# An RWKV-7 and S5 block on one core: the scan's chain as full 128x128 products, its outputs made four chunks at once

## The chip, the cores and the metric

The kernel runs on one NeuronCore of a Trainium2 chip. A NeuronCore has a matrix engine, TensorE (PE in the profile; PEld is its loading of weights), and four more: VectorE (DVE), ScalarE (ACT), GpSimd (POOL) and SyncE (SP). Each works through its own list of instructions in order, and semaphores make one wait for another. DMA queues move data between device memory (DRAM) and the on-chip memory SBUF; matrix products land in a second memory, PSUM, which has eight banks. Each is organised in 128 partitions. The metric is the device time of one execution in microseconds (us); lower is better.

## The reference, cut to what matters

The block normalises x (2048 frames of 1024 channels), projects it, and runs two branches, an RWKV-7 recurrence (16 heads of 64) and an S5 state-space scan (32 groups). Both are gated, projected back, merged, projected once more and added to x. The change touches the RWKV-7 recurrence alone:

```python
def frame_step(S, inp):
    r_t, w_t, k_t, v_t, a_t, b_t = inp
    sa = jnp.einsum('bhij,bhj->bhi', S, a_t)
    S = S * w_t[:, :, None, :] + sa[..., None] * b_t[:, :, None, :] + v_t[..., None] * k_t[:, :, None, :]
    return S, jnp.einsum('bhij,bhj->bhi', S, r_t)
...
_, y = lax.scan(chunk_step, S0, (to_chunks(r), to_chunks(w), to_chunks(k),
                                  to_chunks(v), to_chunks(a), to_chunks(b)))
```

Here w is the decay of each frame and channel, a is minus the normalised key and b is that key times a learned rate.

## The kernel before

**Tiles.** Frames are cut into four blocks of 512 (`tb`), heads into eight pairs (`p`). One *unit* is a pair in a block: channels of the two heads on the 128 partitions (first head on 0 to 63, second on 64 to 127, `HS`), 512 frames along the free axis. There are 32 units; two neighbouring ones are the same pair in two blocks that follow each other. A unit has eight chunks of 64 frames.

**The chunk form.** Within a chunk the recurrence becomes matrix products. `prep1` (L677) makes, per unit, the exponentials of the summed log decay `eg` and of its negative `en`, the columns `BK` (keys divided by the decay) and `AR` (a and r times the decay; r's part in columns C to 2C, L733, on POOL), and `dec`, the decay over the whole chunk. `prep2` (L811) multiplies BK and AR into the matrices A (L822), which ACT and DVE scale and mask into `AT` (L828 to L830). Part of A is a unit triangular matrix per head and chunk; its inverse is needed. The 32x32 diagonal blocks go through DRAM (`ld`, L835, then `IX`, L840, so that all blocks lie side by side on the partitions) and are solved by 62 dependent DVE steps (`solve`, L869 to L877, L872 and L876 in turn). The result goes through DRAM again (`rd`, `R64`, L889 to L894), and the off-diagonal block is put together with 32x32 products (`pz` L908, `pr` L919). `BT`, the transposed BK (L846 to L849), and `SU`, which holds the values v and later the state (L851 to L862), are made in between.

**The scan.** `scan` (L925) then walks through the eight chunks, three steps each:

1. `px` (L934): AT times the current column block `cur` of SU, one full 128x128 product; DVE copies it to `rh`; ACT makes `us`, the state times the chunk's decay (L939).
2. The first half of the output `po` (L943, the state times r), then `pu` (L946), R64 times rh. Both are done head by head as 64x64 products on a quarter of the array each. DVE scales pu for the first head and ACT for the second, back into cur (L947, L948).
3. `pn` (L952), BT times cur, per head a product of 128 rows and 64 columns; two DVE instructions add it to us and write the state into the next chunk's block of SU (L960). Then the second half of the output (L962), AT times cur, per head.

All these operands are float32, and the profile shows each such product as two passes (two weight loads and two matmuls). The unit's output po is one PSUM bank; ACT copies it to `y` (L743, `post1`) at the next unit's start.

**The order of work.** Every engine's list is written by hand through generators. The loop at L1523 takes the units in turn; unit n's scan, the prep2 of unit n + 1, the prep1 of unit n + 2 (from slot 13 on) and the normalisation of unit n - 1 run side by side in 24 *slots* (L1543). A slot emits, in this order, one step of the scan, one step of prep2 (from slot 1 on), DVE work that was put off, then `sums` and prep1, and at last a group of six GEMM matmuls of the big projections (`stream`; slots 1, 9, 15 and 21 take twelve). Before, prep2 puts the two halves of A in slots 1 and 2, IX's loads and the first half of BT in slot 3, the second half of BT in slot 4, SU in slot 5, the solve in slots 6 to 16, pz in slot 22 and pr in slot 23. The solve's steps are woven between the other DVE instructions: `dve` is a wrapper that emits one solve step after every other DVE instruction while some are due (six per slot), so the listing shows many DVE instructions under L75, the line of the wrapper. `sums` (L759) sends row sums through DRAM in slots 4 and 7: `sd` (L771, L774), `cmp` (L777), `rkb`, all issued on SP, as ld, IX, rd and R64 are. Weight loads and several stores are issued on POOL.

PSUM tiles tagged "m" share three banks in turn; A, the transposes of BK, sums, SU's product, pz and pr take them in the order in which they are emitted. `u1` tiles have one buffer each, `up` tiles two, AR three.

Of the kernel before, what the change touches and what calls it, by code (L numbers as in the profile page):

```python
# [81 lines left out]
def tile_rwkv7_s5_block(  # L82
# [181 lines left out]
    if True:  # L264
# [412 lines left out]
        def prep1(p, tb):  # L677
# [50 lines left out]
            dve.tensor_copy(dec, c3(eg)[:, :, C - 1:C])  # L728
            ar = up.tile([P, NC, 2 * C], F32, tag="AR", bufs=3, name="AR" + n)
# [4 lines left out]
            u.update(rk=kh, dec=dec, dd=dd, bk=bk, ar=ar)  # L734
# [76 lines left out]
        def prep2(p, tb):  # L811
# [4 lines left out]
            ld = drx.tile([2, 2, NC, 32, 32], F32, tag="ld", name="ld" + n)  # L816
            for c2 in range(NC // 4):
# [19 lines left out]
            ix = u1.tile([P, 32, 32], F32, tag="IX", name="IX" + n)  # L837
# [3 lines left out]
            bt = up.tile([P, NC, 2, C], F32, tag="BT", name="BT" + n)  # L841
            for c2 in range(NC // 4):
                pb = psm.tile([P, 4, P], F32, tag="m", name=f"pb{n}_{c2}")
                cs_ = slice(4 * c2, 4 * c2 + 4)
                for i in range(4):
                    pe.transpose(pb[:, i, :], bk[:, 4 * c2 + i, 0:2, :].rearrange("p a s -> p (a s)"), ident)  # L846
                act.copy(bt[:, cs_, 0, :], pb[:, :, 0:C])
# [68 lines left out]
            for c in range(NC):  # L916
                for h in range(2):
                    s0 = 64 * h
                    pe.matmul(pr[s0:s0 + 32, 32 * c:32 * c + 32], zt[s0 + 32:s0 + 64, c, :], r64[s0 + 32:s0 + 64, c, 32:64], start=True, stop=True)  # L919
            for h in range(2):  # L920
                s0 = 64 * h
                act.copy(r64[s0:s0 + 32, :, 32:64], pr[s0:s0 + 32, 0:256].rearrange("p (c t) -> p c t", t=32))
            yield

        def scan(p, tb):  # L925
# [4 lines left out]
            for c in range(NC):  # L930
# [6 lines left out]
                us = sm.tile([P, C], F32, tag="us", name=f"us{n}_{c}")  # L937
# [3 lines left out]
                oc = po[:, c * C:(c + 1) * C]  # L941
                for h in range(2):
                    pe.matmul(oc[HS[h]], cur[HS[h], HS[h]], ar[HS[h], c, C:2 * C], start=True, stop=False)  # L943
                pu = pst.tile([P, 512], F32, tag="st", name=f"pu{n}_{c}")
                for h in range(2):
                    pe.matmul(pu[HS[h], 0:C], r64[HS[h], c, :], rh[HS[h], HS[h]], start=True, stop=True)  # L946
                dve.tensor_scalar(out=cur[0:64, 0:64], in0=pu[0:64, 0:C], scalar1=dd[0:64, c:c + 1], scalar2=None, op0=ALU.mult)  # L947
                act.activation(out=cur[64:128, 64:128], in_=pu[64:128, 0:C], func=AF.Copy, scale=dd[64:128, c:c + 1])  # L948
                yield
                pn = pst.tile([P, 512], F32, tag="st", name=f"pn{n}_{c}")  # L950
                for h in range(2):
                    pe.matmul(pn[HS[h], 0:C], bt[:, c, h, :], cur[:, HS[h]], start=True, stop=True)  # L952
                for h in range(2):
                    if c + 1 < NC:
                        nxt = su[HS[h], c + 1, HS[h]]
                    elif tb % 2 == 0:
                        nxt = U[p, tb + 1]["su"][HS[h], 0, HS[h]]
                    else:
                        nxt = ust[HS[h], p, :]
                    (raw_dve if h == 0 else dve).scalar_tensor_tensor(out=nxt, in0=pn[HS[h], 0:C], scalar=dec[HS[h]], in1=us[HS[h]], op0=ALU.mult, op1=ALU.add)  # L960
# [548 lines left out]
        with tc.manual_schedule():  # L1509
# [13 lines left out]
            for n in range(-1, NU + 1):  # L1523
# [180 lines left out]
```

## Time and profile before

| what | us |
|---|---|
| median of 3 runs | 2703.61 |
| lowest and highest | 2698.28 and 2709.49 |
| profiled execution, its own time | 2703.94 |
| span of that execution on the core | 2702.2 |
| first and last px of the scan (L934) | 144.9 and 2085.8 |

The scan's units run from 144.9 to 2085.8 us of the span; before them lies the first normalisation, behind them the S5 branch and the output projections, which the change leaves as they are. A row of the profile names line, engine, operation, out<-in by the program's names and shapes; behind the bar of a group stand busy time in us, mean ns of one, and idle time of the engine just before it with what ended it. In rows by order of time the first two columns are start and duration in us; matmuls overlap, so what one costs is read from the starts, not from the durations. The granted clock of PE was 0.991 of full speed in this execution. The rows themselves stand with the prediction.

### The profile page before, as it was taken

What the parts mean: (1) busy time and instruction counts of PE and PEld (TensorE: products, weight loads), DVE (VectorE), ACT (ScalarE), POOL (GpSimd) and SP (SyncE); (2) the same over time, 40 slices, a digit from 0 to 9 for tenths busy, and PEclk for the clock granted to TensorE, in tenths of its full rate; (3) what the DMA queues carried; (4) which work ended last, traced back from release to release, by engine and by line L of the source; (5) the groups of instructions that cost most, each with busy time, mean ns of one, the idle gap of its engine ahead of it and who ended that gap; (6) DMA issues with size and microseconds to landing.
All of it is one profiled execution on the core that took longest, in us unless ns stands there. A gap on an engine that the chain in (4) does not pass through costs nothing. (4 is left out here: it accounts for less than half of the span.)

```text
span 2702.2 us, 49102 instructions
## 1 busy us (share of the span) xinstructions
PE 2593.4 (96%) x17164; PEld 1970.5 (73%) x17164; DVE 1906.8 (71%) x5620; ACT 1413.6 (52%) x3547; POOL 613.0 (23%) x987
## 2 busy tenths in 40 slices
PE   6999999999999989999999999999989899899998
PEld 5777777777777766777777777777757777677787
DVE  5666777777667777767777767777768789645644
ACT  6456555555556676555555555555644444423321
POOL 2222212122222333222212122221332200111110
PEclk9999999999999999999999999999999999999999
DMA  3232333232333543333323233232466756845533
GB/s 112 79 81 69 97 82 98 72 91 77 89 85 86 138 126 102 92 79 85 85 78 90 80 94 88 78 93 78 133 178 188 218 152 165 247 164 172 169 104 98
DMA packets 256350, 303.54 MB, mean 112 GB/s; under 512 B 159745, under 2 KB 172134, under 8 KB 255078
## 3 DMA queue, kind: packets, MB, share of 16 engines
q1 hardware_dynamic: 210502, 150.94, 20.8%
q0 software_dynamic: 45600, 149.46, 18.7%
q8 instruction: 135, 2.21, 0.3%
q14 instruction: 113, 0.93, 0.1%
HBM read 219.91 MB, written 71.70 MB: 108 GB/s over the span
## 5 line engine op out<-in xcount | busy, mean ns | idle before, releaser
L948 ACT ACTIVATE SU<-pu,dd 64x64 f32<-64x64 f32 x256 | 79.0, 309 | 352.4 <-DVE SU L75 289.4
L872 DVE TENSOR_TENSOR TM<-RF,IX 128x60 f32<-128x60 f32 (+24 forms) x992 | 230.2, 232 | 27.7 <-DMA IX<-ld 5.4
L876 DVE TENSOR_TENSOR RF<-RF,TM 128x60 f32<-128x60 f32 (+24 forms) x992 | 223.9, 226 | 28.3
L939 ACT ACTIVATE us<-SU,dec 64x64 f32<-64x64 f32 x512 | 176.1, 344 | 66.1 <-DVE SU L960 58.2
L75 DVE TENSOR_TENSOR AT<-A,amask 64x256 f32<-64x256 f32 (+1 forms) x256 | 102.3, 419 | 115.0 <-ACT AT L828 109.5
L75 DVE TENSOR_SCALAR SU<-pu,dd 64x64 f32<-64x64 f32 x256 | 69.9, 273 | 112.0 <-PE pu L946 110.2
L828 ACT ACTIVATE AT<-A,dd 64x64 f32<-64x64 f32 x512 | 116.5, 302 | 38.5 <-PE A L822 36.5
L952 PEld LDWEIGHTS pn<-SU,BT 128*64 128x64 f32 x1024 | 56.1, 134 | 104.7 <-issue 38.8
L934 PEld LDWEIGHTS px<-SU,AT 128*128 128x128 f32 x512 | 94.7, 189 | 41.9 <-DVE SU L75 22.0
L960 DVE SCALAR_TENSOR_TENSOR SU<-pn,dec,us 64x64 f32<-64x64 f32 x240 | 65.5, 273 | 79.6 <-PE pn L952 77.6
L943 PEld LDWEIGHTS po<-AR,SU 64*64 64x64 f32 x1024 | 49.8, 131 | 97.0 <-issue 82.5
L75 DVE COPY rh<-px 128x128 f32<-128x128 f32 x256 | 73.9, 289 | 63.9 <-PE px L934 59.7
L488 PE MATMUL ppa<-yhi,whi_pa 128*128 128x512 f32 x256 | 114.1, 446 | 2.2 <-DVE sg L75 1.2
L934 PE MATMUL px<-SU,AT 128*128 128x128 f32 x512 | 100.3, 278 | 14.4 <-DVE SU L75 14.3
L488 PE MATMUL pmb<-hhi,whi_mb 128*128 128x512 f32 x256 | 111.7, 436 | 0.0
L488 PE MATMUL pma<-hhi,whi_ma 128*128 128x512 f32 x256 | 111.1, 434 | 0.0
L488 PE MATMUL pga<-hhi,whi_ga 128*128 128x512 f32 x256 | 110.9, 433 | 0.0
L488 PE MATMUL pk<-hhi,whi_k 128*128 128x512 f32 x256 | 110.8, 433 | 0.0
L488 PE MATMUL pr<-hhi,whi_r 128*128 128x512 f32 x256 | 110.5, 432 | 0.0
L488 PE MATMUL pv<-hhi,whi_v 128*128 128x512 f32 x256 | 109.7, 429 | 0.6 <-ACT carry L441 0.6
L490 PE MATMUL ppa<-yhi,wlo_pa 128*128 128x512 f32 x256 | 102.9, 402 | 2.6 <-DVE wlo_pa L75 2.6
L1662 PE MATMUL pout<-wohi,mhi 128*128 128x512 f32 x256 | 101.1, 395 | 2.5 <-ACT mhi L255 2.4
(374 smaller groups left out, 7980.0 us busy)
## 6 DMA issues: line engine op xcount, KB each, us to landing
IX<-ld SPq DMA_DIRECT2D x128, 128.0 KB
raw_pa<-in_p_a_dram POOLq DMA_DIRECT2D x64, 256.0 KB, 4.5
raw_mb<-in_w_in_dram POOLq DMA_DIRECT2D x50, 256.0 KB, 3.6
raw_r<-in_w_in_dram POOLq DMA_DIRECT2D x36, 256.0 KB, 3.7
raw_k<-in_w_in_dram POOLq DMA_DIRECT2D x36, 256.0 KB, 3.8
raw_v<-in_w_in_dram POOLq DMA_DIRECT2D x36, 256.0 KB, 3.4
raw_ga<-in_w_in_dram POOLq DMA_DIRECT2D x34, 256.0 KB, 3.5
ce<-cw SPq DMA_DIRECT2D x16, 514.0 KB
```

Of the source, the lines that this page charges most:

```text
L75: r = f(*a, **kw)
L488: pe.matmul(ps, hi[:, k, :], xhi[:, kk_, :], start=(kk_ == 0), stop=False)
L490: pe.matmul(ps, lo[:, k, :], xhi[:, kk_, :], start=False, stop=(kk_ == 7))
L828: act.activation(out=at[HS[h], c, 0, h, :], in_=pas[h][HS[h], i, 0:C], func=AF.Copy, scale=dd[HS[h], c:c + 1])
L872: raw_dve.tensor_tensor(out=tm[:, 0:na, 0:nt], in0=rf[:, 0:na, s:s + 1].to_broadcast([P, na, nt]), in1=ix[:, s:s + 1, s + 1:32].to_broadca ...
L876: raw_dve.tensor_tensor(out=rf[:, 0:na, s + 1:32], in0=rf[:, 0:na, s + 1:32], in1=tm[:, 0:na, 0:nt], op=ALU.add)
L934: pe.matmul(px[:, 0:P], at[:, c, 0].rearrange("p h t -> p (h t)"), cur, start=True, stop=True)
L939: act.activation(out=us[HS[h]], in_=cur[HS[h], HS[h]], func=AF.Copy, scale=dec[HS[h]])
L948: act.activation(out=cur[64:128, 64:128], in_=pu[64:128, 0:C], func=AF.Copy, scale=dd[64:128, c:c + 1])
L952: pe.matmul(pn[HS[h], 0:C], bt[:, c, h, :], cur[:, HS[h]], start=True, stop=True)
L960: (raw_dve if h == 0 else dve).scalar_tensor_tensor(out=nxt, in0=pn[HS[h], 0:C], scalar=dec[HS[h]], in1=us[HS[h]], op0=ALU.mult, op1=ALU.add)
L1662: pe.matmul(ps, mhi[:, k, js], whi[:, k, qs], start=(k == 0), stop=False)
```

## The change

- **pu and pn** become one full 128x128 product each, for both heads. R64 gets a block per head, [128, 8, 2, 64], with zeros outside the blocks; two fixed tiles, zeroed once at the start, take the place of the two buffers and of two POOL memsets per unit. DVE and ACT read the diagonal blocks of pu and pn.
- **The outputs** leave the scan. A new function `outs` makes them for four chunks in slot 22 and for the other four in slot 23, after prep2's step: first eight 64x64 products (the state half), then eight of 128x64, each as two passes. For this the state of every chunk must be kept: us, the state times the chunk's decay, goes into the a part of AR instead of a tile of its own, and r's part of AR is divided by that decay. `rdec` (copied on POOL in prep1) is the reciprocal; one POOL product over 128x512 in prep2, in slot 4, applies it.
- **prep2's order**: both halves of BT come first, in slot 1; the two halves of A move to slots 2 and 3, with ld; IX's loads and the POOL product are in slot 4. IX now shares BK's buffer.

```diff
+        r64s = [up.tile([P, NC, 2, C], F32, tag=f"R64{i}", bufs=1, name=f"R64{i}") for i in range(2)]
+        for t_ in r64s:
+            pool.memset(t_, 0.0)
...
+            rdec = sm.tile([P, NC, 1], F32, tag="rdec", name="rdec" + n)
+            pool.tensor_copy(rdec, c3(en)[:, :, C - 1:C])
...
+            bt = up.tile([P, NC, 2, C], F32, tag="BT", name="BT" + n)
+            for c2 in range(NC // 4):
+                pb = psm.tile([P, 4, P], F32, tag="m", name=f"pb{n}_{c2}")
...
+            yield
             for c2 in range(NC // 4):
                 pas = [psm.tile([P, 4, 2 * C], F32, tag="m", name=f"A{n}_{c2}_{h}") for h in range(2)]
...
-            ix = u1.tile([P, 32, 32], F32, tag="IX", name="IX" + n)
+            ix = u1.tile([P, 32, 32], F32, tag="BK", name="IX" + n)
             ldf = ld.rearrange("h b c s t -> (h b c) s t")
             for q in range(4):
                 sp.dma_start(out=ix[32 * q:32 * q + 32], in_=ldf)
-            bt = up.tile([P, NC, 2, C], F32, tag="BT", name="BT" + n)
-            for c2 in range(NC // 4):
...
-                yield
+            pool.tensor_tensor(out=ar[:, :, C:2 * C], in0=ar[:, :, C:2 * C], in1=u["rdec"].to_broadcast([P, NC, C]), op=ALU.mult)
+            yield
...
-            r64 = up.tile([P, NC, C], F32, tag="R64", name="R64" + n)
+            r64 = r64s[units.index((p, tb)) % 2]
...
-                    sp.dma_start(out=r64[s0:s0 + 32, :, 32 * b:32 * b + 32], in_=rd[h, b].rearrange("c a q t -> (a q) c t"))
-                pool.memset(r64[64 * h + 32:64 * h + 64, :, 0:32], 0.0)
+                    sp.dma_start(out=r64[s0:s0 + 32, :, h, 32 * b:32 * b + 32], in_=rd[h, b].rearrange("c a q t -> (a q) c t"))
...
-                us = sm.tile([P, C], F32, tag="us", name=f"us{n}_{c}")
+                us = ar[:, c, 0:C]
...
-                oc = po[:, c * C:(c + 1) * C]
-                for h in range(2):
-                    pe.matmul(oc[HS[h]], cur[HS[h], HS[h]], ar[HS[h], c, C:2 * C], start=True, stop=False)
                 pu = pst.tile([P, 512], F32, tag="st", name=f"pu{n}_{c}")
-                for h in range(2):
-                    pe.matmul(pu[HS[h], 0:C], r64[HS[h], c, :], rh[HS[h], HS[h]], start=True, stop=True)
...
+                pe.matmul(pu[:, 0:P], r64[:, c].rearrange("p h t -> p (h t)"), rh, start=True, stop=True)
...
-                for h in range(2):
-                    pe.matmul(pn[HS[h], 0:C], bt[:, c, h, :], cur[:, HS[h]], start=True, stop=True)
+                pe.matmul(pn[:, 0:P], bt[:, c].rearrange("p h j -> p (h j)"), cur, start=True, stop=True)
...
-                for h in range(2):
-                    pe.matmul(oc[HS[h]], cur[:, HS[h]], at[:, c, 1, h, :], start=False, stop=True)
...
+        def outs(p, tb, cs):
+            u = U[p, tb]
+            ar, at, su, po = (u[k] for k in ("ar", "at", "su", "po"))
+            for c in cs:
+                for h in range(2):
+                    pe.matmul(po[HS[h], c * C:(c + 1) * C], ar[HS[h], c, 0:C], ar[HS[h], c, C:2 * C], start=c == cs[0], stop=False)
+            for c in cs:
+                for h in range(2):
+                    pe.matmul(po[HS[h], c * C:(c + 1) * C], su[:, c, HS[h]], at[:, c, 1, h, :], start=False, stop=c == cs[-1])
...
+                    if sc is not none and slot in (22, 23):
+                        outs(*units[n], range(4 * (slot - 22), 4 * (slot - 21)))
```

More of the change, by code (lines that the diff above doesn't have):

```diff
@@ L733, in prep1 @@
             pool.tensor_tensor(out=ar[:, :, C:2 * C], in0=c3(r), in1=c3(eg), op=ALU.mult)
-            u.update(rk=kh, dec=dec, dd=dd, bk=bk, ar=ar)
+            u.update(rk=kh, dec=dec, rdec=rdec, dd=dd, bk=bk, ar=ar)
             DONE["r"] += 1
@@ L816, in prep2 @@
             ld = drx.tile([2, 2, NC, 32, 32], F32, tag="ld", name="ld" + n)
+            bt = up.tile([P, NC, 2, C], F32, tag="BT", name="BT" + n)
+            for c2 in range(NC // 4):
+                pb = psm.tile([P, 4, P], F32, tag="m", name=f"pb{n}_{c2}")
+                cs_ = slice(4 * c2, 4 * c2 + 4)
+                for i in range(4):
+                    pe.transpose(pb[:, i, :], bk[:, 4 * c2 + i, 0:2, :].rearrange("p a s -> p (a s)"), ident)
+                act.copy(bt[:, cs_, 0, :], pb[:, :, 0:C])
+                for h in range(2):
+                    act.copy(bt[HS[1 - h], cs_, 1, :], pb[HS[h], :, C:2 * C])
+            yield
             for c2 in range(NC // 4):
@@ L840, in prep2 @@
                 sp.dma_start(out=ix[32 * q:32 * q + 32], in_=ldf)
-            bt = up.tile([P, NC, 2, C], F32, tag="BT", name="BT" + n)
-            for c2 in range(NC // 4):
[L843 to L847, printed above, removed]
-                for h in range(2):
-                    act.copy(bt[HS[1 - h], cs_, 1, :], pb[HS[h], :, C:2 * C])
-                yield
+            pool.tensor_tensor(out=ar[:, :, C:2 * C], in0=ar[:, :, C:2 * C], in1=u["rdec"].to_broadcast([P, NC, C]), op=ALU.mult)
+            yield
             su = up.tile([P, NC, P], F32, tag="SU", name="SU" + n)
@@ L901, in prep2 @@
             for h in range(2):
-                dve.transpose(t11[64 * h:64 * h + 32], r64[64 * h:64 * h + 32, :, 0:32])
+                dve.transpose(t11[64 * h:64 * h + 32], r64[64 * h:64 * h + 32, :, h, 0:32])
                 yield
@@ L918, in prep2 @@
                     s0 = 64 * h
-                    pe.matmul(pr[s0:s0 + 32, 32 * c:32 * c + 32], zt[s0 + 32:s0 + 64, c, :], r64[s0 + 32:s0 + 64, c, 32:64], start=True, stop=True)
+                    pe.matmul(pr[s0:s0 + 32, 32 * c:32 * c + 32], zt[s0 + 32:s0 + 64, c, :], r64[s0 + 32:s0 + 64, c, h, 32:64], start=True, stop=True)
             for h in range(2):
                 s0 = 64 * h
-                act.copy(r64[s0:s0 + 32, :, 32:64], pr[s0:s0 + 32, 0:256].rearrange("p (c t) -> p c t", t=32))
+                act.copy(r64[s0:s0 + 32, :, h, 32:64], pr[s0:s0 + 32, 0:256].rearrange("p (c t) -> p c t", t=32))
             yield
@@ L959, in scan @@
                         nxt = ust[HS[h], p, :]
-                    (raw_dve if h == 0 else dve).scalar_tensor_tensor(out=nxt, in0=pn[HS[h], 0:C], scalar=dec[HS[h]], in1=us[HS[h]], op0=ALU.mult, op1=ALU.add)
+                    (raw_dve if h == 0 else dve).scalar_tensor_tensor(out=nxt, in0=pn[HS[h], HS[h]], scalar=dec[HS[h]], in1=us[HS[h]], op0=ALU.mult, op1=ALU.add)
+                yield
+        def outs(p, tb, cs):
+            u = U[p, tb]
+            ar, at, su, po = (u[k] for k in ("ar", "at", "su", "po"))
+            for c in cs:
                 for h in range(2):
-                    pe.matmul(oc[HS[h]], cur[:, HS[h]], at[:, c, 1, h, :], start=False, stop=True)
-                yield
+                    pe.matmul(po[HS[h], c * C:(c + 1) * C], ar[HS[h], c, 0:C], ar[HS[h], c, C:2 * C], start=c == cs[0], stop=False)
+            for c in cs:
+                for h in range(2):
+                    pe.matmul(po[HS[h], c * C:(c + 1) * C], su[:, c, HS[h]], at[:, c, 1, h, :], start=False, stop=c == cs[-1])
         MU, AD, SU = ALU.mult, ALU.add, ALU.subtract
```

4 lines of the change are left out of this document (2 added, 2 removed).

## The prediction

> **What bounds the kernel now.** I read the page's head and its busy times first, then a table by stretches, then the order of time inside one unit.
>
> ```profile
> span 2702.2 us, 49102 instructions
> PE 2593.4 (96%) x17164; PEld 1970.5 (73%) x17164; DVE 1906.8 (71%) x5620; ACT 1413.6 (52%) x3547; POOL 613.0 (23%) x987
> L872 DVE TENSOR_TENSOR TM<-RF,IX 128x60 f32<-128x60 f32 (+24 forms) x992 | 230.2, 232 | 27.7 <-DMA IX<-ld 5.4
> L876 DVE TENSOR_TENSOR RF<-RF,TM 128x60 f32<-128x60 f32 (+24 forms) x992 | 223.9, 226 | 28.3
> ```
>
> PE is busy 96% of the span, so on the whole its instructions are the bound. The average hides one stage. I took the unit that starts at 1661.34 us and cut its 24 slots in three: slots 0 to 5, slots 6 to 20 (the solve of the next unit and what follows it), slots 21 to 23. A row gives the stretch, its length, then busy time and count of PE, weight loads, DVE, ACT and POOL, the granted clock and the DMA's.
>
> ```profile
> 1661.34:1678.98 17.64, 17.64 (x131) 13.10 (x130) 7.86 (x21) 12.51 (x38) 3.88 (x11) 1.00 0.48 128
> 1678.98:1711.78 32.80, 32.75 (x206) 24.18 (x204) 27.71 (x100) 16.17 (x35) 10.16 (x13) 1.00 0.33 90
> 1711.78:1719.99 8.21, 8.21 (x107) 6.37 (x106) 6.01 (x15) 4.36 (x10) 0.79 (x1) 1.00 0.13 35
> ```
>
> The unit takes 58.65 us. PE is full in all three stretches; DVE has room in the first (7.86 of 17.64), but in the middle it is busy 27.71 of 32.80. The 62 solve steps (L872, L876) each hang on the one before; their groups show 27.7 + 28.3 us of idle time, less 5.4 of loads, which is 1.6 us in each of 32 units. So 29.3 of the 32.8 us are DVE's own. Two engines bound the middle stretch together.
>
> **The change on PE.** What a group of the scan costs between two GEMM matmuls is read from start times.
>
> ```profile
> 1687.35 0.40 PE L490 MATMUL pma<-hhi,wlo_ma 128*128 128x512 f32 x1
> 1687.67 0.33 PE L943 MATMUL po<-AR,SU 64*64 64x64 f32 x4
> 1687.84 0.28 PE L946 MATMUL pu<-rh,R 64*64 64x64 f32 x4
> 1688.05 0.50 PE L488 MATMUL pma<-hhi,whi_ma 128*128 128x512 f32 x1
> 1688.38 0.40 PE L489 MATMUL pma<-hlo,whi_ma 128*128 128x512 f32 x1
> ...
> 1698.12 0.39 PE L490 MATMUL pma<-hhi,wlo_ma 128*128 128x512 f32 x1
> 1698.35 0.38 PE L934 MATMUL px<-SU,AT 128*128 128x128 f32 x2
> 1698.49 0.48 PE L488 MATMUL pma<-hhi,whi_ma 128*128 128x512 f32 x1
> 1698.81 0.40 PE L489 MATMUL pma<-hlo,whi_ma 128*128 128x512 f32 x1
> ...
> 1714.57 0.39 PE L490 MATMUL pr<-hhi,wlo_r 128*128 128x512 f32 x1
> ...
> 1715.27 0.69 PE L908 MATMUL pz<-T,AT 32*32 32x32 f32 x32
> 1715.89 0.50 PE L488 MATMUL pr<-hhi,whi_r 128*128 128x512 f32 x1
> 1716.22 0.40 PE L489 MATMUL pr<-hlo,whi_r 128*128 128x512 f32 x1
> ```
>
> A GEMM matmul follows the one before after 0.23 us (1698.12 to px). From 1687.35 to 1688.38 there are two such steps, 0.46, and 0.57 us that the tiled group of eight passes costs: entry 0.09 (0.32 less 0.23), two fours at 0.17, and on the way out 0.04 and 0.10. The full product px costs 1698.81 - 1698.12 - 0.46 = 0.23. In the slot with pz the tiled group costs less, as it shares entry and exit with another tiled group: 1716.22 - 1714.57 - 0.46 = 1.19, of which pz alone would take 0.09 + 0.62 + 0.10 = 0.81, so 0.38.
>
> Per unit, before: 16 tiled groups, 12 at 0.57 and 4 at 0.38 (beside the two A groups, pz and pr), 8.4 us. After: 16 full products, which I price like px, 16 x 0.23 = 3.7; and the outputs, twice 16 passes of 64x64 and 16 of 128x64, each 16 at 4 x 0.17 = 0.68, with two changes of tile shape at 0.04, like the group's way out (1687.84 to 1688.05 is 0.21, less 0.17): twice 1.44 = 2.9. PE saves 8.4 - 6.6 = 1.8 us a unit, 57 us in 32 units. By stretch: slots 0 to 5, two groups from 0.38 and two from 0.57 to 0.23: -1.0. Slots 6 to 20, ten from 0.57 to 0.23: -3.4. Slots 22 and 23: each +1.44 + 0.23 - 0.38: +2.6.
>
> The rows above are what a full and a tiled product cost here. The Trainium skill, TensorEngine Tiling (Array Packing), Theoretical Speedup, speaks against the change: it gives small products up to 2x from tiling and so none to full ones. Its Key Properties say that a change of tiling mode drains the engine, which speaks for it. The trace agrees with both: four tiled passes take 0.17 against 0.23, and entry and exit cost 0.23. By the first alone the unit would lose 6.6 - 16 x 0.34 = 1.2 us, 37 us in all.
>
> **The change on DVE and the queues.** DVE's list stays: same copies, scalings and updates, same shapes. So in slots 6 to 20 it can come forward only by the pauses in which it waits for PE. In this unit they are, up to slot 20:
>
> ```profile
> 1688.17 0.28 DVE L75 TENSOR_SCALAR SU<-pu,dd 64x64 f32<-64x64 f32 x1 [0.52 <-PE pu L946]
> ...
> 1702.03 0.28 DVE L75 TENSOR_SCALAR SU<-pu,dd 64x64 f32<-64x64 f32 x1 [0.43 <-PE pu L946]
> ...
> 1706.64 0.29 DVE L75 COPY rh<-px 128x128 f32<-128x128 f32 x1 [0.25 <-PE px L934]
> ...
> 1710.30 0.28 DVE L960 SCALAR_TENSOR_TENSOR SU<-pn,dec,us 64x64 f32<-64x64 f32 x1 [0.87 <-PE pn L952]
> ```
>
> They sum to 2.1 us (the last figures in brackets). As each slot's PE product needs the DVE result of the slot before, PE gains about 2.0 of its 3.4, and waits for DVE for the rest. I take 2.0; the ends are 1.0 (a unit with fewer pauses) and 3.4.
>
> The second question is whether DVE can start the solve earlier at all. The triangle blocks go through DRAM (ld, then IX), and A, which makes them, moves from slots 1 and 2 to 2 and 3.
>
> ```profile
> 1667.91 1.16 PE L822 MATMUL A<-AR,BK 64*128 64x128 f32 x16
> ...
> 1670.50 0.38 PE L934 MATMUL px<-SU,AT 128*128 128x128 f32 x2
> ...
> 1673.62 1.76 SPq L840 DMA_DIRECT2D IX<-ld  x4
> 1675.43 0.29 SPq L771 DMA_DIRECT2D sd<-rows  x1
> ...
> 1679.28 0.34 SPq L777 DMA_DIRECT2D cmp<-sd  x1
> ...
> 1680.57 0.18 DVE L872 TENSOR_TENSOR TM<-RF,IX 128x31 f32<-128x31 f32 x1
> ...
> 1681.69 0.16 DVE L75 TENSOR_SCALAR cmp<-cmp 128x8 f32<-128x8 f32 x1
> ...
> 1969.96 1.72 SPq L840 DMA_DIRECT2D IX<-ld  x4
> ...
> 1974.02 0.19 DVE L872 TENSOR_TENSOR TM<-RF,IX 128x31 f32<-128x31 f32 x1 [0.89 <-DMA IX<-ld]
> ```
>
> In the new order the second A follows px of slot 3. That px stands at 1670.50; slots 0 to 2 lose one A (1.1) and get both transposes of BK (about 1.0) and save 0.3 in the scan, so A starts near 1670.3, 2.3 us later than 1667.91. The ld and IX issues follow: IX from 1675.9 to 1677.7. The last unit, where DVE did wait for IX, gives the landing: 1974.02 - 1969.96 - 1.72 = 2.3 us after the last issue. So IX is there at 1680.0, while DVE, 1.0 earlier, would want it at 1679.6. Behind IX on SP stand sd and cmp, which reads sd back: sd now goes at 1677.7 instead of 1675.43, and with a landing like IX's cmp goes at 1677.7 + 0.3 + 2.3 = 1680.3, 1.0 later than 1679.28. DVE comes to it in order and found it there at 1681.69. Both waits stand in front of the scan's work on DVE. I count DVE's start as neither earlier nor later than before: slots 0 to 5 give nothing. The ends are 1.0 earlier and 0.5 later.
>
> What is left: POOL gets the rescaling of AR, one 128x512 product like L733, and a copy of 8 columns, and loses two memsets of R.
>
> ```profile
> L943 PE MATMUL po<-AR,SU 64*64 64x64 f32 x1024 | 84.8, 242 | 3.4 <-ACT y L743 3.4
> ...
> L733 POOL TENSOR_TENSOR AR<-zr,eG 128x512 f32<-128x512 f32 x32 | 42.3, 1321 | 2.0
> ...
> 1688.88 1.76 DVE L876 TENSOR_TENSOR RF<-RF,TM 128x76 f32<-128x76 f32 x1
> 1689.24 1.29 POOL L791 TENSOR_TENSOR rkb<-rkb,zv 128x512 f32<-128x512 f32 x1
> ```
>
> That is 1.3 us a unit, the copy and the memsets about even, on an engine that is busy 3.88 of 17.64 there, before DVE's solve; at nothing, and 1.3 if that cover goes (below). It waits for the second A to have read AR; behind it on POOL stand SU's copy, RF's memsets and DMA issues, all for slot 6 or later. ACT's copies of BT come in slot 1, its count stays; us goes to AR instead of its own tile, same shape. IX in BK's buffer waits for PE's last read of BK, before the ld that it waits for anyway; the next BK is written after the solve. R's loads wait for pu of two units before, as now. po's first product waited 3.4 us in all for the copy y; written from slot 22 on, it will not. y itself, on ACT in slot 0, waits for the outputs of slot 23, which end six GEMM matmuls (1.4 us) before; behind it on ACT is us, wanted two slots later.
>
> **Sum.** Gain at slot 21: 2.0. Slots 22 and 23: 2.6 more, with no DVE bound to hide in. So +0.6 us a unit, for 31 units with a next solve: +18; less 2 for the last unit, which has none beside it: +16. The wait of po is left out, as PE would spend it waiting for DVE. The profiled execution took 2703.94 us (span 2702.2, 1.7 around it; the median shown is 2703.61): 2720 us, +0.6%. A measurement here tells about 0.5% from no change, 13.5 us.
>
> **The rivals.**
> *PE alone decides.* The change does what it says: DVE gives way, and PE's 57 us and po's 3 come off: 2644. For it: PE is full everywhere. Against it: 29.3 us of DVE work stand in a stretch that would shrink to 29.4, and each pause would have to fall right. This is the case on the other side; it decides if DVE's pauses add up to over 3 us and IX lands before DVE wants it.
> *Loads in time, DVE bound.* IX and cmp land early enough, so slots 0 to 5 give their 1.0: -0.4 a unit, 2691. For it: in the page DVE waited for IX 5.4 us in all. Against: IX used to be there at 1673.62 + 1.76 + 2.3 = 1677.7, 2.9 us before 1680.57, and the two shifts (2.3 and 1.0) take 3.3.
> *POOL holds DVE.* In the rows above an L876 step, 0.23 otherwise, took 1.76 us while POOL ran a two-input product. If the rescaling falls into DVE's full stretch, each unit pays 1.3 more: 31 x 1.3 = 40, 2760. Against: it is issued two slots before the solve. The Trainium skill, GPSIMD Engine Reference, Specifications, says that the SBUF interface is shared and that DVE instructions with two SBUF inputs contend; the trace agrees, by that row.
>
> **How the numbers follow.** DVE paced by late loads, 2705 to 2742: 0.39. PE alone, 2640 to 2680: 0.27, as PE is the engine that is full throughout. Loads in time, 2680 to 2705: 0.26. POOL holds DVE, 2742 to 2775: 0.08. The range leaves out the lowest third of the second and most of the last: 2653 to 2748. Faster by over 0.5% (under 2690): the second and a third of the third, 0.36. Slower (over 2717): 0.08 and 0.27 of the first, 0.35. Between: 0.29.
>
> **What would show it.** Right: the groups of pu and pn at 0.23 between GEMM matmuls, the unit's slots 22 and 23 longer by 2.6, idle time of PE before px, pu and pn ended by DVE in slots 7 to 20, and L872 waiting for IX in most units. Wrong: no IX wait, or a middle stretch below 30 us (PE alone); full products dearer than 0.23, or outputs over 1.44 a group, move the sum by 32 us per us and unit.

## The result, and the profile after

| | before | after |
|---|---|---|
| median of 4 runs | 2704.86 | 2784.43 |
| ratio, 95% interval | | 1.0293 (1.0263 to 1.0323) |
| span of the profiled execution | 2702.2 | 2780.0 |
| granted clock of PE | 0.991 | 0.982 |
| start of the first px | 145.10 | 148.47 |
| slots 0 to 5, mean of 31 units | 17.93 | 17.30 |
| slots 6 to 20 | 34.58 | 35.06 |
| slots 21 to 23 | 8.38 | 10.91 |
| a unit | 60.90 | 63.28 |

The kernel became 2.9% slower, 79.6 us by the medians, where 16 had been forecast. The means come from the starts of px's matmuls (144.9, given further up, is px's first weight load): a unit runs from its first px to the next unit's, cut at the px of chunk 2 and of chunk 7. 31 x 2.38 = 73.8 us and 3.4 before the first unit make up 77.2 of the 77.8 us between the spans. Slots 21 to 23 grew by 2.5, near the forecast's 2.6, and slots 0 to 5 fell by 0.6, where nothing had been counted. What failed lies between: slots 6 to 20, which were to become 2.0 us shorter, took 0.5 longer, although PE has 3.4 us less to do there.

The head of the page after, and its groups by line (busy, mean ns, then idle time before them and what ended it):

```profile
span 2780.0 us, 47342 instructions
PE 2577.7 (93%) x16140; PEld 2044.4 (74%) x16140; DVE 1923.0 (69%) x5620; ACT 1409.1 (51%) x3547; POOL 632.4 (23%) x989
...
L879 DVE TENSOR_TENSOR TM<-RF,IX 128x60 f32<-128x60 f32 (+24 forms) x992 | 236.7, 239 | 64.7 <-DMA IX<-ld 42.4 <-DVE RF L883 0.2
...
L953 PE MATMUL pn<-SU,BT 128*128 128x128 f32 x512 | 112.6, 302 | 67.9 <-ACT SU L950 66.0
```

The group of pn before:

```profile
L952 PE MATMUL pn<-SU,BT 128*64 128x64 f32 x1024 | 94.7, 246 | 8.4 <-DVE SU L75 5.8 <-ACT SU L948 0.8
```

PE's share fell from 96% to 93%: it now waits. The solve waits 42.4 us for IX, before 5.4; pn waits 67.9 us, before 8.4. The unit that starts at 1784.86 shows both. Its three stretches, with the columns of the prediction's table:

```profile
1784.86:1801.50 16.64, 16.64 (x107) 13.44 (x106) 8.32 (x22) 12.63 (x39) 2.49 (x7) 1.00 0.25 64
1801.50:1835.56 34.06, 31.55 (x145) 24.87 (x144) 28.98 (x108) 16.12 (x38) 6.52 (x7) 0.95 0.27 68
1835.56:1845.92 10.36, 10.36 (x160) 8.68 (x158) 7.76 (x15) 6.21 (x15) 2.81 (x5) 1.00 0.36 114
```

In the middle PE stands still for 34.06 - 31.55 = 2.5 us, and its clock is 0.95. In order of time, SP's queue first, then DVE, ACT and PE:

```profile
1795.74 2.52 SPq L850 DMA_DIRECT2D ld<-AT  x4
1801.47 1.71 SPq L855 DMA_DIRECT2D IX<-ld  x4
...
1805.52 0.34 SPq L782 DMA_DIRECT2D cmp<-sd  x1
...
1807.07 1.23 SPq L668 DMA_DIRECT2D lraw<-in_w_up_dram  x2
1808.34 1.23 SPq L668 DMA_DIRECT2D lraw<-in_a_up_dram  x2
...
1805.55 0.19 DVE L879 TENSOR_TENSOR TM<-RF,IX 128x31 f32<-128x31 f32 x1 [2.32 <-DMA IX<-ld]
...
1811.37 0.41 ACT L675 CAST lhi<-lraw 128x256 fp32r<-128x256 f32 x1 [1.94 <-DMA lraw<-in_a_up_dram]
...
1807.12 0.49 PE L953 MATMUL pn<-SU,BT 128*128 128x128 f32 x2 [2.22 <-ACT SU L950]
```

IX's four issues end at 1803.18, 18.3 us into the unit (14.0 in the unit of the prediction), and land 2.4 us later; DVE stands for 2.32. Behind its late solve steps stands the scaling of pu, behind that ACT's, behind that pn: PE stands for 2.22. Then lraw, behind all that on SP, comes too late for ACT, and lora_lo on DVE with it.

### The profile page after: what moved, and what is told of

The parts are those of the page before. It is cut to its first block, busy times and chain, and to the rows that moved or that the text cites. A ratio compares the mean times of both kernels' runs of the same rounds, so it can differ in the third digit from the quotient of the medians.

```text
span 2780.0 us, 47342 instructions
## 1 busy us (share of the span) xinstructions
PE 2577.7 (93%) x16140; PEld 2044.4 (74%) x16140; DVE 1923.0 (69%) x5620; ACT 1409.1 (51%) x3547; POOL 632.4 (23%) x989
## 3 DMA queue, kind: packets, MB, share of 16 engines
q0 software_dynamic: 45600, 149.46, 18.1%
## 5 line engine op out<-in xcount | busy, mean ns | idle before, releaser
L879 DVE TENSOR_TENSOR TM<-RF,IX 128x60 f32<-128x60 f32 (+24 forms) x992 | 236.7, 239 | 64.7 <-DMA IX<-ld 42.4
L883 DVE TENSOR_TENSOR RF<-RF,TM 128x60 f32<-128x60 f32 (+24 forms) x992 | 217.2, 219 | 28.6 <-DVE TM L879 0.4
L945 ACT ACTIVATE AR<-SU,dec 64x64 f32<-64x64 f32 x512 | 176.2, 344 | 75.3 <-DVE SU L961 67.7
L953 PEld LDWEIGHTS pn<-SU,BT 128*128 128x128 f32 x512 | 86.4, 191 | 130.2 <-ACT SU L950 119.4
L953 PE MATMUL pn<-SU,BT 128*128 128x128 f32 x512 | 112.6, 302 | 67.9 <-ACT SU L950 66.0
L961 DVE SCALAR_TENSOR_TENSOR SU<-pn,dec,AR 64x64 f32<-64x64 f32 x240 | 65.3, 272 | 116.7 <-PE pn L953 116.5
L948 PEld LDWEIGHTS pu<-rh,R 128*128 128x128 f32 x512 | 92.3, 189 | 57.6 <-DVE rh L75 37.2
L948 PE MATMUL pu<-rh,R 128*128 128x128 f32 x512 | 103.4, 284 | 18.7 <-DVE rh L75 17.7
```

The costliest lines, as they stand in the source:

```text
L879: raw_dve.tensor_tensor(out=tm[:, 0:na, 0:nt], in0=rf[:, 0:na, s:s + 1].to_broadcast([P, na, nt]), in1=ix[:, s:s + 1, s + 1:32].to_broadca ...
L883: raw_dve.tensor_tensor(out=rf[:, 0:na, s + 1:32], in0=rf[:, 0:na, s + 1:32], in1=tm[:, 0:na, 0:nt], op=ALU.add)
L945: act.activation(out=us[HS[h]], in_=cur[HS[h], HS[h]], func=AF.Copy, scale=dec[HS[h]])
L948: pe.matmul(pu[:, 0:P], r64[:, c].rearrange("p h t -> p (h t)"), rh, start=True, stop=True)
L953: pe.matmul(pn[:, 0:P], bt[:, c].rearrange("p h j -> p (h j)"), cur, start=True, stop=True)
```

## The experiments

Each is measured beside the kernel before on the same chip; that had medians of 2701.1 to 2704.9 us. A difference between two experiments is taken from their ratios to it (0.001 is 2.7 us), and their two intervals leave it 5 to 10 us either way. Two theories to begin with: **L**, the late loads are what the middle stretch lost; **N**, pn as one product must wait for both heads' scaling.

### The order of prep2: e1, e2, e5

e1 is the changed kernel with A first again (a line in brackets stands for several of the code):

```diff
-            (both halves of BT)
-            yield
             for c2 in range(NC // 4):
                 pas = [...]
...
+            (both halves of BT)
             ix = u1.tile([P, 32, 32], F32, tag="BK", name="IX" + n)
             (IX's loads)
+            yield
             pool.tensor_tensor(out=ar[:, :, C:2 * C], ...)
```

> The changed kernel with the two halves of A back in slots 1 and 2 (ld in slot 2); both halves of BT and IX's loads in slot 3, the POOL product in slot 4. Theory L (late loads: A's move delays ld, IX, sd, cmp and lraw on SP, and that is what the middle stretch lost): the pauses of the solve for IX (1.2 us a unit on the mean) and the pauses of the scan behind cmp and lraw (about 0.5 a unit) go, 31 x 1.7 = 53 us: about 2731 us, and the group TM<-RF,IX shows under 10 us of idle time for IX. Theory N (pn as one product must wait for both heads' scaling, DVE's and then ACT's): the waits of pn stay at 60 to 70 us, the loads were only in part on the path, and at most 20 us go: 2765 or more.

Measured: **2715.43** (ratio to before 1.0056, 1.0039 to 1.0074), 64 us less than the changed kernel. Its groups:

```profile
span 2713.5 us, 47344 instructions
...
L879 DVE TENSOR_TENSOR TM<-RF,IX 128x60 f32<-128x60 f32 (+24 forms) x992 | 238.2, 240 | 25.9 <-DMA IX<-ld 3.7
...
L953 PE MATMUL pn<-SU,BT 128*128 128x128 f32 x512 | 109.4, 295 | 34.6 <-ACT SU L950 32.7
```

Theory L holds, and half of what pn waited for was the late solve. e2 is the kernel before with the new order alone (BT in slot 1, A in 2 and 3, IX's loads in 4):

> The kernel before with nothing but the new order of prep2: both halves of BT in slot 1, the halves of A in slots 2 and 3, IX's loads in slot 4 (IX keeps its own buffer). The predicted step (the loads land as late as DVE would want them, no loss): within 10 us of the kernel before, 2695 to 2715. Theory L: each unit loses what the changed kernel's solve waits for IX, 1.2, and about 0.5 for cmp and lraw, 31 x 1.7 = 53: 2758, and IX's pauses rise from 5 us to over 30. Theory N: the order costs at most 20 us: 2725 or less.

Measured: **2744.18** (1.0152, 1.0133 to 1.0171): 41 us for the order alone, less than theory L's 2758; the solve's wait for IX rose from 5.4 to 28.3 us. The longer slots 0 to 5 let DVE come to IX later there: the order starts the solve 1.0 us later than before (20.24 against 19.25 us into the unit, in the mean of ordinary units), and in the changed kernel 1.3 us later than in e1 (19.75 against 18.48).

The three waits can be added up over 31 units: IX 36.4 us after against 0.7 in e1, cmp 8.7 against 0.5, lraw 18.1 against 6.4, together 55.6; the 31 units differ by 56.5 us (1961.6 and 1905.1). That the two agree so well doesn't show that each wait costs its length: IX and cmp hold DVE, lraw holds ACT. e5 takes out one of the three by an earlier issue:

```diff
-                        if slot == 5:
+                        if slot == 2:   # at the head of the slot
                             lraw = lora_dma(a[0])
```

> The changed kernel (late order kept), but the loads of lraw issued in slot 2 instead of slot 5, so that on SP they stand ahead of ld and IX. Theory Q (the order costs by three separate waits for loads; in the changed trace 36 us for IX, 9 for cmp, 18 for lraw): lraw's 18 us fall below 4, IX and cmp stay, in the 15 units concerned about 0.8 us comes off each: 2784 - 12 = 2772. Rival C (the waits hide each other: DVE comes to lora_lo late anyway, the pause moves to another wait): 2784 within 5 us.

Measured: **2771.63** (1.0258, 1.0243 to 1.0274), about 10 us less, with 0 to 19 inside the intervals. lraw's wait fell to 0.4 us and IX's (36.4) and cmp's (7.3) stayed, as theory Q has it, but the 31 units of the trace became only 4.4 us shorter (1957.2): not all of lraw's 18 us stood on the path, and rival C isn't ruled out.

### Full products and batched outputs, each alone: e3, e4, e6, e15

e3 (late order) and e15 (A first) make pu and pn head by head, with the outputs batched as changed:

```diff
-                pe.matmul(pu[:, 0:P], r64[:, c]..., rh, start=True, stop=True)
+                for h in range(2):
+                    pe.matmul(pu[HS[h], HS[h]], r64[HS[h], c, h, :], rh[HS[h], HS[h]], start=True, stop=True)
...
-                pe.matmul(pn[:, 0:P], bt[:, c]..., cur, start=True, stop=True)
+                for h in range(2):
+                    pe.matmul(pn[HS[h], HS[h]], bt[:, c, h, :], cur[:, HS[h]], start=True, stop=True)
```

> The changed kernel with pu and pn again head by head (two tiled products each, the first head of pn needs DVE's scaling alone); outputs, order and rescaling stay as changed. Theory N: the waits of pn fall from 68 us to under 15 and DVE's chain runs as before, so the middle stretch loses them: 45 to 60 us less, about 2730. Theory L: pn's waits are only where the late start of DVE shows, the time stays within 15 us of 2784. If PE were the bound in the middle stretch: 10 groups of 0.34 us more, 31 x 3.4 = 105 us more, 2889; half of that if PE's waits there take up half.

> e1_a_first (2715) with pu and pn head by head again, outputs still batched. On PE a tiled group of four alone costs 0.09 + 0.17 + 0.14 = 0.40, a full product 0.23: 0.17 x 14 slots outside 22 and 23 = 2.4 us a unit, of it 0.7 in slots 0 to 5. If PE's time counts everywhere: 31 x 2.4 = 74, 2789. If PE's waits of 1.2 to 1.5 us in slots 6 to 20 take up theirs: 31 x (0.7 + 0.3) = 31, 2746. Theory N (the pair pays for its wait for both scalings, 33 us on pn): 2715 or less.

Measured: e3 **2795.10** (1.0350, 1.0323 to 1.0376), 15 us more than the changed kernel; e15 **2753.29** (1.0179, 1.0163 to 1.0195), 33 us more than e1. Theory N falls as the main cause: pn's waits did shrink in e3 (to 27 us), but slots 6 to 20 took the same 35.0 us a unit, with ten dearer groups on PE. Where DVE waits for loads, PE's saving is mostly spent waiting (15 us are left of it); where it doesn't, full products are worth 33. What the wait for both scalings costs by itself stays open, as head by head PE has more to do.

e4 (late order) and e6 (A first) have the full products, but make the outputs in the scan as before:

```diff
-                us = ar[:, c, 0:C]
+                us = sm.tile([P, C], F32, tag="us", name=f"us{n}_{c}")
...
+                oc = po[:, c * C:(c + 1) * C]
+                for h in range(2):
+                    pe.matmul(oc[HS[h]], cur[HS[h], HS[h]], ar[HS[h], c, C:2 * C], start=True, stop=False)
                 (pu)
...
+                    pe.matmul(oc[HS[h]], cur[:, HS[h]], at[:, c, 1, h, :], start=False, stop=True)
```

> The changed kernel with full products for pu and pn and the new order, but the outputs made in the scan as before, chunk by chunk (us in its own tile again; the POOL rescaling is left out as it is not needed). Slots 22 and 23 then lose two groups of 1.44 us and gain back two of about 0.4: 2.1 a unit, 65 us: 2719, if DVE hides the outputs' groups in slots 6 to 20. If PE is the bound there, the tiled groups, two of three slots at 0.23 for entry and exit and 0.17 more, 10 x 0.4 = 4 us a unit, come back on the path: 2784 - 65 + 124 = 2843. In between, as PE has 2 to 4 us of waits a unit in that stretch: 2740 to 2780.

> Full products for pu and pn alone: prep2 in the old order (A in slots 1 and 2, IX and BT in slot 3), outputs in the scan as before, us in its own tile, no rescaling. By the prices of the prediction: before, the outputs and pu or pn shared one tiled group at 0.57; now 0.23 for the full product and 0.17 + 0.23 for the tiled four alone, 0.63: 16 x 0.06 = 1.0 us a unit more on PE, 31 us: about 2732 against 2701 before. Theory N (pn waits for both scalings) adds PE's waits for pn, 20 to 30 us: 2755. If DVE hides PE's part in slots 6 to 20: 2705 to 2715.

Measured: e4 **2802.21** (1.0375, 1.0357 to 1.0393), e6 **2780.80** (1.0286, 1.0269 to 1.0302). e6 lies 77 us over before, where 31 had been expected. PE in order of time:

```profile
1700.74 0.40 PE L493 MATMUL pv<-hhi,wlo_v 128*128 128x512 f32 x1
1700.98 0.38 PE L955 MATMUL pn<-SU,BT 128*128 128x128 f32 x2
1701.29 0.34 PE L965 MATMUL po<-AT,SU 128*64 128x64 f32 x4
1701.56 0.51 PE L491 MATMUL pma<-hhi,whi_ma 128*128 128x512 f32 x1
1701.90 0.40 PE L492 MATMUL pma<-hlo,whi_ma 128*128 128x512 f32 x1
```

The pair of full product and tiled four takes 1701.90 - 1700.74 - 0.46 = 0.70 us, not 0.63; two tiled fours took 0.57. 16 x 0.13 = 2.1 us a unit, 65 us in 31; the means of a unit differ by 2.4 (63.30 against 60.90); it fits that four of the 16 groups had cost only 0.38 before. So neither half of the change pays alone: full products give up the mode that the outputs' fours then enter by themselves, and only the batch takes those entries away (e6 to e1: 62 us; in the late order, e4 to the changed kernel, 22).

### What is left of e1: e7, e8, e16

e16 leaves the rescaling out:

> e1_a_first (2715) without the POOL product that rescales AR (the outputs' state half is then off by the chunk's decay). The prediction's step, at nothing: 2710 to 2717. If it holds DVE or delays POOL's work behind it in front of the solve: up to 1.3 us a unit, 31 x 1.3 = 40, 2675.

Measured: **2721.02** (1.0056, 1.0038 to 1.0075), the ratio of e1: it costs nothing that these runs can tell (7 us either way). e7 and e8, both on e1:

```diff
# e7
-                    if sc is not none and slot in (22, 23):
-                        outs(*units[n], range(4 * (slot - 22), 4 * (slot - 21)))
+                    if sc is not none and slot in (13, 23):
+                        outs(*units[n], range(4 * (slot == 23), 4 + 4 * (slot == 23)))
# e8
-                dve.tensor_scalar(out=cur[0:64, 0:64], in0=pu[0:64, 0:64], scalar1=dd[0:64, c:c + 1], scalar2=None, op0=ALU.mult)
+                act.activation(out=cur[0:64, 0:64], in_=pu[0:64, 0:64], func=AF.Copy, scale=dd[0:64, c:c + 1])
```

> The changed kernel with A first (as e1_a_first, 2715), and the outputs of the first four chunks made in slot 13 instead of slot 22; those of the last four stay in slot 23. Slot 22 loses 1.44 + 0.23 - 0.38 = 1.3 us, 31 x 1.3 = 40. Theory D (DVE sets the pace of slots 6 to 20, where PE waits 1.2 to 1.9 us a unit in e1_a_first's trace): the group of 1.67 us goes into PE's waits, and 30 to 40 us come off: 2675 to 2685. Theory P (PE's waits there are too short and in other slots, the group is paid in full): 31 x 0.37 = 11 us more, 2726. Half of it hidden: 2700.

> The changed kernel with A first, and pu's scaling for both heads on ACT (two instructions of 0.31 us) instead of one on DVE and one on ACT. Theory D (DVE's chain sets slots 6 to 20): DVE loses 8 instructions of 0.27 us and its pauses for pu (98.8 us in e1_a_first's trace, 3.1 a unit), up to 31 x 1.5 = 46 us come off until PE is full: about 2670. Theory N (pn's wait for ACT is the tight place): ACT now has two instructions in a row, 0.3 later than the pair was if it followed DVE anyway by 0.4: pn's waits stay at 35 us and the time at 2705 to 2720. If ACT is held by its long instructions (0.6 to 0.7 us casts) before it gets to the scaling, pn waits longer and the time goes above 2725.

Measured: e7 **2723.11** (1.0079, 1.0064 to 1.0094), e8 **2709.46** (1.0037, 1.0019 to 1.0055). e7 pays for the group in full: slots 21 to 23 become 0.75 us a unit shorter and slots 6 to 20 0.74 longer, so PE's waits there (0.8 to 3.2 us in an ordinary unit) are no room for other work. Nor does DVE's length make most of them on this base: with 2.2 us less on DVE a unit some 5 us come off, which is within the noise. Cut slot by slot, e1's trace shows why: about 1.0 us of the wait stands in one slot of every unit (10 or 11). DVE, POOL and PE there:

```profile
1703.38 0.24 DVE L883 TENSOR_TENSOR RF<-RF,TM 128x76 f32<-128x76 f32 x1
1703.66 2.01 DVE L879 TENSOR_TENSOR TM<-RF,IX 128x72 f32<-128x72 f32 x1
...
1704.25 1.31 POOL L796 TENSOR_TENSOR rkb<-rkb,zv 128x512 f32<-128x512 f32 x1
...
1706.59 0.46 PE L940 MATMUL px<-SU,AT 128*128 128x128 f32 x2 [1.00 <-DVE SU L75]
```

It is the row that the prediction showed for a rival: a solve step held up by a POOL product (the hold, from here on). Before, it was there too, and in most units PE had work enough to cover it: in slots 10 and 11 of units 15 to 28 it waits 0.2 us at most on the mean, and 1.0 in one of them in e1. In the even units 2 to 12 the cover was missing before, too: there it waited 0.8 to 1.3 us.

### The POOL product out of the solve: e9 to e14, e17, e18

```diff
# e9, e10, e11, e12: slot 22; e13, e14: slot 1, and e17, e18: slot 4 of the next unit
-                    if slot in (3, 4, 6 if last else 7, 11):
+                    if slot in (3, 4, 6 if last else 7, 22):
                         next(sg, None)
```

> e1_a_first (A first; 2715), with the POOL product rkb x v moved from slot 11 to slot 22, past the solve. In e1_a_first's trace one solve step takes 2.0 us while that product runs (1.31 us on POOL), and the one slot in which PE waits 1.0 us in every unit follows it. Theory H (PE's shorter list no longer covers that hold): PE's wait there goes, 31 x 1.0 = 31 us less: about 2684, below the kernel before. Theory C (PE and DVE pass the wait on: it comes back in the next slots, as they hold each other all through slots 6 to 20): 2705 to 2715.

> The kernel before with the same move of the POOL product from slot 11 to slot 22. Theory H: there PE's longer list covers the hold, PE waits only 0.04 to 0.2 us a unit in those slots: 1 to 8 us less, 2694 to 2701. If the hold cost the kernel before as much as the changed one: 31 us less, 2671.

> e8_act_scales_both (A first, both scalings on ACT; 2709) with the POOL product in slot 22. Theory H: 31 x 1.0 us less: about 2678. If ACT's scalings and the product cured the same wait: no better than e9_product_late.

> e11_act_and_product with the outputs of the first four chunks in slot 13, as in e7. With DVE freed of 2.2 us and of the hold, PE is full in slots 6 to 20, and the 1.67 us group is paid there for 1.3 saved in slot 22: 31 x 0.4 = 11 us slower than e11. Theory D (DVE still leaves PE waits that the group fills): up to 20 us faster than e11.

| | base | median | ratio to before |
|---|---|---|---|
| e9 | e1, product in slot 22 | 2708.95 | 1.0020 (1.0008 to 1.0032) |
| e10 | before, slot 22 | 2690.65 | 0.9955 (0.9943 to 0.9968) |
| e11 | e8, slot 22 | 2688.42 | 0.9948 (0.9931 to 0.9965) |
| e12 | e11, half of the outputs early | 2691.50 | 0.9956 (0.9942 to 0.9970) |

With the product moved no solve step takes over 0.25 us in e9 and e10; the longest had been 2.0 us before and 2.1 in e1.

e10 gained 12 us, more than theory H's 1 to 8: the hold had cost the kernel before something as well, and of the 9.9 us that its 31 units gain 7.7 stand in the even units 2 to 12. e11 suggests that DVE's length counts for more once the hold is gone: both scalings on ACT, worth about 5 us in e8, are worth 20 from e9 to e11. e12 equals e11 within the intervals: slots 21 to 23 become 0.9 us a unit shorter and slots 6 to 20 0.8 longer, so there too the moved group is paid for.

e9 gained about 10 us of 31. Slots 6 to 20 did lose 32.5 us (1035.2 to 1002.7 over 31 units), but slots 21 to 23 took back 24, above all in the odd units of the first half. One of them, DVE and PE, then stretches of the same time (length, busy of PE, PEld, DVE, ACT, POOL, granted clock, DMA):

```profile
376.01 3.08 DVE L75 TENSOR_SCALAR AR<-zk,pd 128x8 f32<-128x8 f32 x1
...
379.48 0.49 PE L948 MATMUL pu<-rh,R 128*128 128x128 f32 x2 [2.09 <-DVE rh L75]
```

```profile
370.00:377.00 7.00, 7.00 (x34) 5.40 (x33) 6.64 (x15) 3.47 (x8) 1.34 (x3) 1.00 0.25 54
377.00:379.50 2.50, 0.41 (x3) 0.03 (x1) 2.44 (x3) 0.00 (x0) 2.06 (x2) 1.00 0.34 105
379.50:381.00 1.50, 1.50 (x36) 1.31 (x38) 1.47 (x4) 0.11 (x1) 0.00 (x0) 0.62 0.00 0
381.00:383.00 2.00, 2.00 (x32) 1.79 (x32) 1.30 (x3) 1.23 (x5) 0.00 (x0) 0.50 0.02 4
383.00:385.00 2.00, 2.00 (x7) 1.59 (x6) 0.00 (x0) 1.70 (x3) 0.00 (x0) 0.50 0.00 0
385.00:387.00 2.00, 2.00 (x37) 1.58 (x35) 0.55 (x2) 0.00 (x0) 0.00 (x0) 0.58 0.00 0
387.00:389.00 2.00, 2.00 (x45) 1.74 (x40) 1.31 (x3) 1.29 (x4) 0.00 (x0) 1.00 0.04 8
```

Two POOL products, AR's and the moved one, stood behind each other; DVE's instruction took 3.08 us, PE stood for 2.09, and then its clock was about half for 7 us, worth 1.5 x 0.38 + 2 x 0.5 + 2 x 0.5 + 2 x 0.42 = 3.4 us more. It is the dearest of six such pauses: after four the clock was half for about 3.4 us, worth 1.7, and after one not at all. In e1, at the same place, PE stands for 0.86 and the clock stays at 1.00:

```profile
379.00:381.00 2.00, 1.14 (x36) 0.98 (x37) 1.91 (x5) 0.00 (x0) 0.45 (x1) 1.00 0.30 111
381.00:383.00 2.00, 2.00 (x37) 1.73 (x37) 1.69 (x5) 0.99 (x4) 0.00 (x0) 1.00 0.02 4
```

e13 (on e1) and e14 (on e8) move the product on, to slot 1:

> e1_a_first (2715) with the POOL product rkb x v moved from slot 11 to slot 1 of the next unit, where DVE is idle for 2.5 of 4.3 us and POOL has no other product. Theory H (the hold, uncovered by PE's shorter list, cost 1.0 us a unit; in e9 it came back only because two POOL products stood one behind the other in slots 20 to 22, and the clock fell after pauses of 2.1 us): the middle stretch falls by 1.0 as in e9, slots 21 to 23 stay at 10.4 to 11.5: 2715 - 31 = 2684. Theory C (what PE gains in slots 6 to 20 is lost again to DVE at the next slots): 2705 to 2715, as e9.

> e8_act_scales_both (2709) with the product in slot 1 of the next unit. Theory H: 2709 - 31 = 2678, and less clock lost than e11's. Theory C: as e11, 2688.

Measured: e13 **2698.55** (0.9984, 0.9974 to 0.9994), e14 **2683.11** (0.9920, 0.9907 to 0.9932). The middle stretch fell further (e13: 993.3), but slots 21 to 23 kept the 25 us. In POOL's queue of e13 the cause is plain:

```profile
374.27 0.75 POOL L217 DMA_DIRECT2D raw_gb<-in_w_in_dram  x1 [7.26 <-DVE wlo_ga L75]
...
375.19 1.27 POOL L738 TENSOR_TENSOR AR<-zr,eG 128x512 f32<-128x512 f32 x1
376.42 1.25 POOL L796 TENSOR_TENSOR rkb<-rkb,zv 128x512 f32<-128x512 f32 x1
```

POOL had stood behind a DMA issue, came late to AR's product, and had the moved one, whose inputs were long there, next in its list: a later slot doesn't hold an instruction back. Slot 4 does, behind the rescaling, which waits for A. e17 is e14 so mended, and e18 the kernel before with the same two edits (it has no rescaling, so there slot 4 alone places the product):

> e14_act_and_slot1 (2683) with the moved product in slot 4 of the next unit, right behind the rescaling of AR on POOL, so that it can't run early behind the product for AR in slots 20 to 22. Theory H: the pauses of 2.1 us at the seven odd units of the first half become the 0.9 of e1_a_first, and with them the half clock behind them: 25 us less of slots 21 to 23, about 2660; the middle stretch stays at 31.6. If two POOL products behind one another hold DVE in front of the solve as well: the solve starts later, up to 1.3 us a unit, 2683 to 2720.

> The kernel before with the same two edits: both scalings of pu on ACT, and the POOL product in slot 4 of the next unit. As PE is full there (e10, 2691, with the product alone moved), DVE's relief buys little: 2685 to 2692. If the edits are worth as much here as in the changed kernel (2715 to 2683): 2670.

Measured: e17 **2676.65** (0.9888, 0.9867 to 0.9909), e18 **2685.00** (0.9919, 0.9905 to 0.9933). In the seven odd units of the first half slots 21 to 23 fell from 97.7 us (e14) to 80.3 (e1: 80.9), but slots 0 to 5 rose by 8.4 over all units. e17 beats the kernel before, by 1.1%, and the changed one. It falls short of theory H's 2660. How much of that is the change, and how much the two edits? e18 gains 0.8% without it. On this base the change, in e1's order, is worth about 8 us, and the spread of five runs each leaves 1 to 15.

## Why the prediction was wrong

**The step that failed** is the one on the loads: "I count DVE's start as neither earlier nor later than before: slots 0 to 5 give nothing. The ends are 1.0 earlier and 0.5 later." Over 27 ordinary units (without 0, 13, 14, 30) the solve starts 19.25 us into the unit before, 18.48 in e1, and 19.75 after: 0.5 later than before, the far end of the bounds, and 1.3 later than it could. Two things made it so. IX's issues end 17.0 us into the unit on the mean (15.7 to 18.9), where one unit's rows had given 16.4; and the landing, taken from one row at 2.3, lies between 2.3 and 3.9. The second A does start where the forecast had it (8.7 us into the unit, forecast 9.0), but it takes 1.55 us in place of 1.16, and from ld's last issue to IX's first 2.0 us pass in place of 1.5.

**What was missed** stands on the same queue: lraw, issued on SP in slot 5 behind all that moved, isn't in the prediction at all. It cost about 10 us (e5, 0 to 19). cmp was there, as a step that DVE would find just in time; it waited 8.7 us. With IX's 36.4 the order cost 64 us in the changed kernel (e1).

**The gain of 2.0 at slot 21** was mis-sized too. e1 has no load waits, its DVE starts 0.8 earlier, and it gains 0.6 in slots 0 to 5 and 1.2 in slots 6 to 20, so 1.0 of DVE's pauses in place of 2.0: the lower end. What held it was the POOL product within the solve, which PE's shorter list covers less: with it gone slots 6 to 20 give 1.0 to 1.35 us a unit more (e9, e13), in the kernel before 0.5 (e10). Between e10 and e13, which both have it out of the solve, slots 0 to 20 differ by 2.8 us a unit; the solve starts 0.8 of that earlier, and the 2.0 that are left are the gain that was forecast. The prediction quoted a row of the hold, but as a danger from the rescaling alone, and priced it for DVE, not for PE's cover. That e1 lies at 2715 and the forecast at 2720 is chance: the one error took the gain at slots 0 to 5 away where e1 has it, the other gave too much behind it.

**The miss in the forecast's own terms** is 1.8 us a unit (2.4 against 0.6). As far as the traces split it, the late start made 0.5 of it, the smaller gain 1.0, and 0.4 is left where cmp and lraw hold the scan up; slots 21 to 23 took off 0.1. So the order cost 64 us against e1, where the solve starts earlier than before, but only about half of the miss against the forecast, which had not counted on that.

**Right** were the prices of the full products on PE. pu between GEMM matmuls after: 1742.77 - 1742.08 - 0.46 = 0.23, as forecast:

```profile
1742.08 0.40 PE L493 MATMUL pma<-hhi,wlo_ma 128*128 128x512 f32 x1
1742.31 0.39 PE L948 MATMUL pu<-rh,R 128*128 128x128 f32 x2
1742.45 0.48 PE L491 MATMUL pma<-hhi,whi_ma 128*128 128x512 f32 x1
1742.77 0.39 PE L492 MATMUL pma<-hlo,whi_ma 128*128 128x512 f32 x1
...
1717.54 0.68 PE L969 MATMUL po<-AR 64*64 64x64 f32 x16
1718.15 0.69 PE L972 MATMUL po<-AT,SU 128*64 128x64 f32 x16
1718.77 0.50 PE L491 MATMUL pga<-hhi,whi_ga 128*128 128x512 f32 x1
```

A batch of outputs took 1.23 us, not 1.44, so an undisturbed unit pays 10.36 - 8.21 = 2.15 in slots 21 to 23 and not 2.6; the mean came to 2.53 by waits in some units (the odd ones of the first half behind AR's product, and units 13 and 14). The rescaling at nothing was right (e16).

**The rivals.** "PE alone decides" came true in single units only, the odd ones of the second half in e17, which take 56.2 to 57.2 us (58.6 to 59.3 before) with PE almost full in slots 6 to 20. One of them:

```profile
1640.05:1656.89 16.84, 16.72 (x108) 13.30 (x107) 7.13 (x18) 12.00 (x37) 6.11 (x13) 1.00 0.46 122
1656.89:1685.98 29.09, 29.09 (x146) 24.11 (x145) 25.42 (x94) 17.00 (x39) 8.52 (x11) 1.00 0.35 100
1685.98:1696.34 10.36, 10.36 (x160) 8.68 (x159) 6.61 (x15) 5.15 (x13) 1.54 (x2) 1.00 0.18 48
```

"Loads in time" is e1, 24 us above its 2691, in large part by the hold (e13, without it: 2699). Open stays why the units 13 and 14, where the two halves of the frames meet, take 6 us more in e17 than before (154.8 against 149.0), and which part of the 64 us the lower clock made: the clock that the trace of the changed kernel shows lost is 2780 x 0.018 = 50 us, of e1's 2713.5 x 0.012 = 33, but a slower PE costs time only where PE is late.

## What to carry to other kernels

When a step is moved, list every transfer that stands behind its transfers on the same queue, with who waits for each, and take landing times from their spread, not from one row. A shorter list on the fullest engine doesn't only save its own time: it uncovers stalls of its neighbour that were there all along (the hold cost slots 6 to 20 0.5 us a unit before, and 1.0 to 1.35 in e1), so look for the single long instance of a short instruction in the neighbour's list before counting the gain. And a later place in the program doesn't delay an instruction whose inputs are ready: in an in-order queue it runs as soon as what stands before it is done.

## What the runs showed of the hardware

A POOL product of two SBUF inputs (1.3 us) held one DVE instruction 2.0 us (no such step takes over 0.25 us in e9, e10, e13 and e17, where the product lies elsewhere), and two such products in a row held one DVE instruction of 8 columns for 3.08 us (median of its 32 instances: 0.37). A pause of PE of 2.09 us was followed by about 7 us at half the granted clock, one of 0.86 us by none. The Trainium skill, TensorE: Matmul & The Clock Gate, Part 1, says that the clock is half after at least one idle window of about 3.4 us and that the windows run freely; of six such pauses of 2.1 us in e9 five were followed by half the clock, and one was not. Its stretches:

```profile
736.60:739.00 2.40, 0.35 (x2) 0.30 (x2) 2.34 (x3) 0.00 (x0) 1.64 (x2) 1.00 0.24 87
739.00:741.00 2.00, 2.00 (x67) 1.76 (x65) 1.97 (x6) 0.24 (x2) 0.00 (x0) 1.00 0.02 4
741.00:743.00 2.00, 2.00 (x24) 1.61 (x24) 0.59 (x2) 1.90 (x5) 0.00 (x0) 1.00 0.04 8
```

That agrees with windows that don't start with the pause, but not with a whole idle window as the condition: here a pause of 2.1 us was enough in five of six cases.
